# A hybrid decoder layer: three more places for raw weights in the seven-product passes, the sums of weights in the convolution's buffers, and a plain pair first

## The chip, the cores and the metric

The kernel runs on one core of one Trainium2 chip. The core's engines each work through a queue of their own in order: TensorE (PE in the profile, its weight loads PEld), VectorE (DVE), ScalarE (ACT), GpSimd (POOL) and SyncE (SP), which here issues nearly all transfers from memory. They are kept in step by semaphores. The metric is the device time of one execution in microseconds, and fewer is better. Three runs of the kernel before gave 1087.1, 1087.87 and 1090.15 us; the median is 1087.87 us.

## The reference

One decoder layer on 256 tokens of width 2048, all in float32. A token mixer (two groups of attention heads and an output projection) comes first; its code is not touched. Then comes the channel mixer, where the change lies:

```python
h = rmsnorm(x, pre_ffn_g[l])
u = causal_dwconv(h @ w_up[l], conv_w[l], conv_b[l])      # w_up 2048 x 11264, conv of width 3
gate, val = jnp.split(u, 2, axis=-1)
y = (jax.nn.gelu(gate, approximate=True) * val) @ w_down[l]   # w_down 5632 x 2048
x = x + rmsnorm(y, post_ffn_g[l])
```

## The kernel before, in words

**Precision.** A float32 matrix is split into a high part (`whi`, a cast by ACT) and a low part (`wlo`, the difference, by DVE), both in the 32-bit format that PE multiplies at full pace. A product of float32 matrices is then three matmuls: high by high, high by low, low by high. A weight comes in by DMA as a `raw` tile of 128 x 1024 (512 KB). There are five such places, taken in turn; a load can be issued only when the last reader of the place's former weights is done. There are likewise five places each for `whi` and `wlo`, free again when PE has read them.

**The channel mixer** runs in two halves of 2816 columns (22 tiles of 128, `FHALF`). In each half the up-projection (`proj_T4`, L272 to L290) makes, 11 times, a pair of tiles of the gate and a pair of the value. `conv` turns each into a convolved tile: ACT copies half of the PSUM bank (L881), DVE adds the other (L882), POOL multiplies with a row of scales (L883), ACT makes the last tap (L885), DVE adds the two others (L887, L889). ACT takes the GELU of the gates (L1033), DVE multiplies gate and value (L1040), and the product is split into `G` (L312 on ACT, L313 on DVE). These buffers (`u`, `cs`, `yg`, `yv`) are separate tiles, taken in turn.

**The seven-product passes** (`fast_pass`, L953 to L1012) multiply `G` by 1024 columns of `w_down`. There are three: two in half 0 (columns 0 to 1023, then 1024 to 2047) and one in half 1 (columns 0 to 1023). A pass has 11 pairs of rows of weights, each pair two loads, `ra` and `rb`. A pair is a 2 x 2 block of tiles by a 2 x 2 block of columns (`left`, `right`), so a plain pair takes eight products, 24 matmuls of 512 columns. The pairs 0, 2, 4 and 6 (`FAST`) are done with seven products, 21 matmuls, over sums of blocks. For these DVE makes `t13` and `t24` in the tile `tb` from `ra` and `rb` with four subtractions (L983, L984, L987, L989), and four parts are then split: half of `ra`, `t13`, `t24` and `rb`. A plain pair needs two splits. PE's matmuls all stand in L951. The eight PSUM banks of a pass are called `early` (four sums of products, done after the last fast pair, added to `y_sb` by `add_early`) and `late` (the four blocks that plain pairs also add to, taken out by `add_late`).

`tb` lies before the change in the room of `gbc` (free) in half 0, and in half 1 in the room of `hT`, which PE reads until the end of the up-projection. The vector `gbc_ffn` (1 MB, needed when the last columns are taken out) lies in `gbc`.

**After the passes** of half 1 come the columns 1024 to 1535 of that half and at last 1536 to 2047, both with three matmuls per product (L309), and the final norm.

**What sets the order.** PE's queue is in the order of the program text. On the other engines a scheduler places the instructions at build time by what they depend on and an estimate of when that is done. Each queue is strict at run time: an instruction that waits holds up all behind it, on SP too.

Of the kernel before, what the change touches and what calls it, by code (L numbers as in the profile page):

```python
# [8 lines left out]
F32 = mybir.dt.float32  # L9
# [8 lines left out]
P = 128  # L18
S = 256
D = 2048  # L20
# [11 lines left out]
def hybrid_layer(ctx: ExitStack, tc: tile.TileContext, x, pre_mix_g, w_in, b_forget, sinks,  # L32
# [814 lines left out]
    with tc.tile_pool(name="ffn", bufs=1) as fp:  # L847
# [23 lines left out]
        ubuf = [fp.tile([P, 258], F32, tag=f"u{i}", name=f"u{i}") for i in range(NU)]  # L871
        for u in ubuf:
            pool.memset(u[:, 0:2], 0.0)
        cnt = [0]
        y_sb = main.tile([P, 2, D], F32, tag="y", name="y_sb")

        def conv(b, ch, dst_tag):
            u = ubuf[cnt[0] % NU]
            cnt[0] += 1
            c = fp.tile([P, 256], F32, tag="cs", bufs=3, name="cs")  # L880
            act.copy(c, b[:, 256:512])  # L881
            dve.tensor_tensor(u[:, 2:258], b[:, 0:256], c, op=ALU.add)  # L882
            pool.tensor_tensor(u[:, 2:258], u[:, 2:258], rowf, op=ALU.mult)  # L883
            y = fp.tile([P, 256], F32, tag=dst_tag, bufs=4, name=dst_tag)
            act.activation(y, u[:, 2:258], AF.Identity, bias=cw[:, 3, ch:ch + 1],  # L885
                           scale=cw[:, 2, ch:ch + 1])
# [66 lines left out]
        def fast_pass(G, sums, k00, c0, tb, early, late, add_early, add_late):  # L953

            left, right = slice(0, 512), slice(512, UNIT)
            pairs = FHALF // 2
            plain = [u for u in range(pairs) if u not in FAST]
# [11 lines left out]
            for u in range(pairs):  # L969
                k = 2 * u  # L970
                ra, rb = (w_load(w_rows(w_down, k00 + k + a, 1, c0, UNIT), 1, UNIT)[0]
                          for a in range(2))
                if u in FAST:
                    i = FAST.index(u)
                    one, end = i == 0, i == len(FAST) - 1
# [7 lines left out]
                    dve.tensor_tensor(t13[:, left], ra[:, right], ra[:, left], op=ALU.subtract)  # L983
# [5 lines left out]
                    dve.tensor_tensor(t24[:, right], rb[:, left], t24[:, left],  # L989
                                      op=ALU.subtract)  # L990
                    f24 = parts(t24, UNIT)
                    b2 = parts(rb, UNIT)
                    product(m1, *of(k, 0), b11, left, one, end)
                    product(m5, *s_of(0), f13, left, one, end)
                    product(m7, *s_of(2), f13, right, one, end)
                    product(m6, *s_of(1), f24, left, one, end)
                    product(p4, *of(k + 1, 1), f24, right, one, False)
                    product(p2, *of(k + 1, 0), b2, left, one, False)
                    product(p3, *s_of(3), b2, right, one, False)
# [5 lines left out]
                end = u == pairs - 1  # L1005
                order2 = ([(a, x) for x in blocks for a in range(2)] if end else
                          [(a, x) for a in range(2) for x in blocks])
                for a, (bk, t, cols) in order2:
                    product(bk, *of(k + a, t), b[a], cols,
                            bk is p22 and u == plain[0] and a == 0, end and a == 1)  # L1010
# [5 lines left out]
        for half in range(2):  # L1016
            G = [fp.tile([P, 512], F32R, tag="G", bufs=FHALF, name=f"G{j}") for j in range(FHALF)]
            sums = None
            for g in range(FHALF // 2):
                c0 = (half * (FHALF // 2) + g) * 256  # L1020
                alt = (g + half) % 2
# [39 lines left out]
            tags = ("acc", "att") if half else ("att", "acc")  # L1061
            tb = (main.tile([P, 4, UNIT * 2], F32, tag="hT", name="tb")[:, 0:2, 0:UNIT] if half else
                  fp.tile([P, 2, UNIT], F32, tag="gbc", name="tb"))
            for n in range(0, 2 if half else 4, 2):
                early, late = ([bank(tag) for _ in range(4)] for tag in tags)
# [30 lines left out]
                fast_pass(G, sums, half * FHALF, n * 512, tb, early, late, add_early, add_late)  # L1096
# [34 lines left out]
        rest = main.tile([P, KT, 512], F32R, tag="hT", name="rest")  # L1131
# [4 lines left out]
        for u in range(FHALF // 2):  # L1136
            if u in (1, 2):
                sp.dma_start(x_back[:, u - 1, :], x_dram[(u - 1) * P:u * P, :])
            hi, lo = w_unit(w_rows(w_down, FHALF + u * 2, 2, 1536, 512), 2, 512,
                            keep=(None, [rest[:, c:c + 2, :].rearrange("p a c -> p (a c)")  # L1140
                                         for c in (4 * (u - LAST), 4 * (u - LAST) + 2)])
# [57 lines left out]
```

## Time and profile before

| what | value |
|---|---|
| median of three runs | 1087.87 us |
| the profiled execution, its own time | 1087.17 us |
| its span in the profile | 1085.4 us |
| PE busy | 1060.9 us, 98% of the span |
| DVE busy | 818.7 us, 75% |
| ACT busy | 630.8 us, 58% |
| POOL busy | 219.7 us, 20% |
| moved by DMA | 207.09 MB, mean 191 GB/s |
| mean granted clock of PE | 0.993 |

Between the span and the execution's own time lie 1.8 us. A busy PE is one that has a matmul under way, not one at its full pace: consecutive matmuls overlap in the records, so a lone matmul shows some 0.39 us where a stream of them takes 0.227 us for each.

### The profile page before, as it was taken

To read this page: it belongs to the slowest core of one execution; us is meant where nothing else is said; L and a number is where in the kernel's file an instruction comes from. 1 tells how busy PE (TensorE), PEld (TensorE's weight loads), DVE (VectorE), ACT (ScalarE), POOL (GpSimd) and SP (SyncE) were. 2 spreads that over 40 slices of the span, in tenths; PEclk is the share of its full clock that TensorE was granted. 3 is DMA by queue.
4 is the path that set the end of the run, shared out by engine and by line. 5 is a ranking of instruction groups with operands and counts; after the bars stand their busy time and mean duration, and the time that the engine had idled before them with its cause. 6 is when DMAs were issued, how large, how long until landed. Compare 5 with 4: busy or idle time off the path is not lost.

```text
span 1085.4 us, 16365 instructions
## 1 busy us (share of the span) xinstructions
PE 1060.9 (98%) x5950; PEld 919.6 (85%) x5950; DVE 818.7 (75%) x1336; ACT 630.8 (58%) x1087; POOL 219.7 (20%) x252
## 2 busy tenths in 40 slices
PE   8999999999999999999999999999999999989996
PEld 6899978887889888888888787888888888868886
DVE  5988878887568877778679887667877777588663
ACT  6766756667547756566565544455656565455550
POOL 3343243332022212121121000011212121100211
PEclk9999999999999999999999999999999999989998
DMA  8645556544862876566664655866666566457752
GB/s 287 207 123 172 175 155 211 166 149 155 306 220 80 290 216 190 181 197 191 193 194 152 195 175 186 298 187 186 191 198 191 179 198 191 135 160 225 278 171 78
DMA packets 157100, 207.09 MB, mean 191 GB/s; under 512 B 6844, under 2 KB 131036, under 8 KB 155996
## 3 DMA queue, kind: packets, MB, share of 16 engines
q1 hardware_dynamic: 156016, 203.37, 59.7%
q10 hardware_dynamic: 1004, 2.68, 0.6%
q8 instruction: 47, 0.77, 0.3%
q14 instruction: 33, 0.27, 0.1%
HBM read 201.68 MB, written 4.21 MB: 190 GB/s over the span
## 4 chain that ended last, share of the span: by engine, by line
PE 83%; DVE 7%; DMA 5%; issue 2%; ACT 2%; POOL 1%; SPq 0%; DVEq 0%; POOLq 0%; ACTq 0%
PE bank_acc L309 18%; PE bank_att L284 15%; PE bank_acc L284 14%; PE bank_att L290 8%; PE bank_acc L290 7%; PE bank_acc L253 5%; PE bank_att L951 5%; PE bank_acc L951 4%; DMA raw<-in_w_down_dram 3%; PE bank_acc L258 3%; DVE wlo L313 2%; DVE wlo L115 1%; PE bank_att L475 1%; PE bank_att L510 1%; PE bank_acc L916 1%
## 5 line engine op out<-in xcount | busy, mean ns | idle before, releaser
L115 DVE TENSOR_TENSOR wlo<-raw,whi 128x1024 fp32r<-128x1024 f32 (+3 forms) x291 | 358.4, 1241 | 136.9 <-ACT whi L112 132.7
L112 ACT CAST whi<-raw 128x1024 fp32r<-128x1024 f32 (+3 forms) x290 | 294.5, 1031 | 151.8 <-issue 91.9
L883 POOL TENSOR_TENSOR u<-u,rowf 128x256 f32<-128x256 f32 x88 | 95.5, 1105 | 497.3 <-DVE u L882 495.6
L284 PE MATMUL bank_att<-hT,whi 128*128 128x512 f32 x704 | 165.7, 390 | 0.0
L284 PE MATMUL bank_acc<-hT,whi 128*128 128x512 f32 x672 | 158.2, 390 | 0.0
L284 PEld LDWEIGHTS bank_att<-hT,whi 128*128 128x128 f32 x704 | 130.5, 188 | 26.3
L284 PEld LDWEIGHTS bank_acc<-hT,whi 128*128 128x128 f32 x672 | 124.5, 188 | 25.0
L253 PE MATMUL bank_acc<-hT,whi 128*128 128x512 f32 x352 | 89.2, 396 | 0.0
L290 PEld LDWEIGHTS bank_att<-hT,wlo 128*128 128x128 f32 x704 | 85.4, 188 | 1.9
L312 ACT CAST whi<-raw 128x1024 fp32r<-128x1024 f32 (+1 forms) x66 | 62.4, 973 | 41.9 <-PE bank_acc L951 14.8
L290 PE MATMUL bank_att<-hT,wlo 128*128 128x256 f32 x704 | 85.7, 279 | 0.0
L951 PE MATMUL bank_acc<-whi,G 128*128 128x512 f32 x264 | 84.7, 389 | 0.0
L290 PEld LDWEIGHTS bank_acc<-hT,wlo 128*128 128x128 f32 x672 | 81.6, 188 | 1.8
L309 PE MATMUL bank_acc<-whi,oT 128*128 128x512 f32 (+1 forms) x272 | 82.5, 380 | 0.0
L290 PE MATMUL bank_acc<-hT,wlo 128*128 128x256 f32 x672 | 82.1, 279 | 0.0
L313 DVE TENSOR_TENSOR wlo<-raw,whi 128x1024 fp32r<-128x1024 f32 (+1 forms) x66 | 73.2, 1132 | 9.3 <-ACT whi L312 9.3
L253 PEld LDWEIGHTS bank_acc<-hT,whi 128*128 128x128 f32 x352 | 62.9, 188 | 11.3
L951 PEld LDWEIGHTS bank_acc<-whi,G 128*128 128x128 f32 x264 | 49.6, 188 | 10.3
L309 PEld LDWEIGHTS bank_acc<-whi,oT 128*128 128x128 f32 x272 | 50.2, 188 | 9.3
L951 PE MATMUL bank_acc<-wlo,G 128*128 128x512 f32 x132 | 52.2, 395 | 2.9 <-DVE wlo L313 2.7
L309 PE MATMUL bank_acc<-whi,G 128*128 128x512 f32 (+1 forms) x196 | 51.8, 350 | 0.0
L309 PE MATMUL bank_acc<-wlo,oT 128*128 128x512 f32 (+1 forms) x136 | 51.2, 377 | 0.0
(249 smaller groups left out, 1664.7 us busy)
## 6 DMA issues: line engine op xcount, KB each, us to landing
raw<-in_w_up_dram SPq DMA_DIRECT2D x176, 512.0 KB, 3.9
raw<-in_w_down_dram SPq DMA_DIRECT2D x88, 512.0 KB, 5.0
raw<-in_w_in_dram SPq DMA_DIRECT2D x51, 512.0 KB, 4.0
raw<-in_w_out_dram SPq DMA_DIRECT2D x32, 512.0 KB, 5.0
raw<-in_w_in_dram SPq DMA_DIRECT2D x16, 384.0 KB, 3.4
cb<-c_dram SPq DMA_DIRECT2D x8, 256.0 KB, 3.7
x_sb<-in_x_dram SPq DMA_DIRECT2D x2, 1024.0 KB
x_dram<-x_sb ACTq DMA_DIRECT2D x2, 1024.0 KB
```

The source lines that it names most:

```text
L112: i1 = act.copy(hi[:, cs], raw[:, cs])
L115: i2 = dve.tensor_tensor(lo[:, cs], raw[:, cs], hi[:, cs].bitcast(F32), op=ALU.subtract)
L253: pe.matmul(b, parts[u][0][:, a, m * P:(m + 1) * P], hT[:, kt, :], start=(kt == 0), stop=(kt == KT - 1))
L258: pe.matmul(b[:, 256:512], parts[u][1][:, a, m * P:(m + 1) * P], hT[:, (v + u) * 4 + a, 0:256], start=False, stop=False)
L284: pe.matmul(b, parts[u][0][:, a, m * P:(m + 1) * P], hT[:, kt, :], start=(kt == 0), stop=(kt == KT - 1))
L290: pe.matmul(b[:, 256:512], parts[u][1][:, a, m * P:(m + 1) * P], hT[:, kt, 0:256], start=False, stop=False)
L309: pe.matmul(b, a, r[:, cols], start=(first and i == 0), stop=(last and i == 2))
L312: act.copy(hi, src)
L313: dve.tensor_tensor(lo, src, hi.bitcast(F32), op=ALU.subtract)
L475: pe.matmul(sb[e][:, cs], a[r, t * P:(t + 1) * P], b[r, 0:nk], start=(n == 0), stop=(n == 2))
L883: pool.tensor_tensor(u[:, 2:258], u[:, 2:258], rowf, op=ALU.mult)
L951: pe.matmul(b, a, r[:, cols], start=(first and i == 0), stop=(last and i == 2))
```

## The change

Six edits go together:

1. All of the convolution's buffers become slices of one tile `room` (4128 floats wide), taken up anew for each half by `conv_room`; `from_ring` deals them out in turn, as many of each as before.
2. When the convolutions of a half are done, the same room is taken up as `tb`, now three rows of 1024: two for `t13` and `t24`, the third a place for raw weights.
3. The room `gbc` becomes `extra`, two more places for raw weights. Of each eight loads of the passes the first five go to `raw`, then two to `extra` and one to `tb`.
4. The first pass of each half (`n == 0`) takes its pairs in the order 1, 0, 3, 2, 5, 4, 7, 6, 8, 9, 10. `first` finds for each bank which product starts it.
5. All passes use the `acc` banks for `early` and `att` for `late`; the alternation of banks in the up-projection of half 1 is shifted to suit.
6. `gbc_ffn` moves into the room of `hT`, and the held weights `rest` of the end move from there to `gbc` and `room`.

```diff
+        def conv_room():
+            room = fp.tile([P, ROOM], F32, tag="room", name="room")
+            ubuf[:] = [room[:, i * 258:(i + 1) * 258] for i in range(NU)]
+            for u in ubuf:
+                pool.memset(u[:, 0:2], 0.0)
+            at = NU * 258
+            for tag, n in (("cs", 3), ("yg", 4), ("yv", 4)):
+                rings[tag] = [room[:, at + i * 256:at + (i + 1) * 256] for i in range(n)]
+                at += n * 256
+
+        def from_ring(tag):
+            r = rings[tag]
+            r.append(r.pop(0))
+            return r[-1]
...
-            c = fp.tile([P, 256], F32, tag="cs", bufs=3, name="cs")
+            c = from_ring("cs")
...
-            y = fp.tile([P, 256], F32, tag=dst_tag, bufs=4, name=dst_tag)
+            y = from_ring(dst_tag)
...
-            for u in range(pairs):
+            for u in order:
                 k = 2 * u
-                ra, rb = (w_load(w_rows(w_down, k00 + k + a, 1, c0, UNIT), 1, UNIT)[0]
-                          for a in range(2))
+                ra, rb = (load(w_rows(w_down, k00 + k + a, 1, c0, UNIT)) for a in range(2))
...
+            if half:
+                conv_room()
             for g in range(FHALF // 2):
                 c0 = (half * (FHALF // 2) + g) * 256
-                alt = (g + half) % 2
+                alt = g % 2
...
-                gbf = fp.tile([P, D], F32, tag="gbc", name="gbc_ffn")
+                gbf = main.tile([P, 4 * D], F32, tag="hT", name="gbc_ffn")[:, 0:D]
                 sp.dma_start(gbf, post_ffn_g[0].partition_broadcast(P))
...
-            tags = ("acc", "att") if half else ("att", "acc")
-            tb = (main.tile([P, 4, UNIT * 2], F32, tag="hT", name="tb")[:, 0:2, 0:UNIT] if half else
-                  fp.tile([P, 2, UNIT], F32, tag="gbc", name="tb"))
+            extra = fp.tile([P, 2, UNIT], F32, tag="gbc", name="extra")
+            tb = fp.tile([P, 3, UNIT], F32, tag="room", name="tb")
+            spare = [extra[:, 0, :], extra[:, 1, :], tb[:, 2, :]]
+            loads = [0]
+
+            def load(src):
+                i = loads[0] % 8
+                loads[0] += 1
+                if i < 5:
+                    return w_load(src, 1, UNIT)[0]
+                sp.dma_start(spare[i - 5].rearrange("p (a c) -> p a c", a=1), src)
+                return spare[i - 5]
+
             for n in range(0, 2 if half else 4, 2):
-                early, late = ([bank(tag) for _ in range(4)] for tag in tags)
+                early, late = ([bank(tag) for _ in range(4)] for tag in ("acc", "att"))
+                order = list(range(FHALF // 2))
+                if n == 0:
+                    order[:8] = [1, 0, 3, 2, 5, 4, 7, 6]
...
-        rest = main.tile([P, KT, 512], F32R, tag="hT", name="rest")
+        rest = [fp.tile([P, 2, UNIT], F32R, tag="gbc", name="rest"),
+                fp.tile([P, ROOM], F32R, tag="room", name="rest")[:, 544:544 + 2 * UNIT]
+                .rearrange("p (a c) -> p a c", a=2)]
```

**How the queues change.** DVE at the start of the third pass (half 1), before: `u`, `yv` are the last convolution, `tb` and `wlo` the first fast pair (lines 983 to 989 the subtractions, 313 the splits). One split of that pair stands ahead of the end of the up-projection.

```order
L313 TENSOR_TENSOR wlo<-raw,whi 128x512
...
L983 TENSOR_TENSOR tb<-raw 128x512
L882 TENSOR_TENSOR u_3941<-bank_att,cs 128x256
L882 TENSOR_TENSOR u_3942<-bank_att,cs 128x256
L984 TENSOR_TENSOR tb<-raw 128x512
L987 TENSOR_TENSOR tb<-raw,tb 128x512
...
L1040 TENSOR_TENSOR yv<-yv,yg 128x256 x2
L313 TENSOR_TENSOR wlo<-tb,whi 128x1024
```

The same place now (898 to 905 are the convolution, 1004 to 1010 the subtractions):

```order
L313 TENSOR_TENSOR wlo<-raw,whi 128x1024
L313 TENSOR_TENSOR wlo<-raw,whi 128x512
L898 TENSOR_TENSOR room<-bank_acc,room 128x256 x2
...
L313 TENSOR_TENSOR G_7350<-room,G_7350 128x256
L1004 TENSOR_TENSOR tb<-raw 128x512
L1005 TENSOR_TENSOR tb<-raw 128x512
L1008 TENSOR_TENSOR tb<-raw,tb 128x512
L1010 TENSOR_TENSOR tb<-raw,tb 128x512
L313 TENSOR_TENSOR wlo<-tb,whi 128x1024 x2
L313 TENSOR_TENSOR wlo<-raw,whi 128x1024 x2
L313 TENSOR_TENSOR wlo<-extra,whi 128x1024
```

The splits of pair 1 and of half a `ra` now stand ahead of the last convolution, and all four subtractions behind the whole of it.

SP at the same place, with the end of the up-projection's loads (`raw<-in_w_up_dram`), one piece of the difference:

```order
-L69 DMA raw<-in_w_down_dram 128x1024 x21
-L1138 DMA x_back<-x_dram 128x2048
-L69 DMA raw<-in_w_down_dram 128x1024
-L69 DMA raw<-in_w_down_dram 128x2x512 x6
-L1138 DMA x_back<-x_dram 128x2048
...
+L1093 DMA extra<-in_w_down_dram 128x1024 x2
+L69 DMA raw<-in_w_up_dram 128x4x256 x87
+L69 DMA raw<-in_w_down_dram 128x1024 x7
+L1072 DMA gbc_ffn<-in_post_ffn_g_dram 128x2048
+L1093 DMA tb<-in_w_down_dram 128x1024
+L69 DMA raw<-in_w_down_dram 128x1024 x3
```

Two of the first eight weights are loaded an up-projection early, and `gbc_ffn` now stands in front of the load into `tb`.

DVE late in the first pass of half 0, now (the second row is the first subtraction of the second pass; the first row splits pair 6; 1109 and 1110 are `add_early`):

```order
L313 TENSOR_TENSOR wlo<-tb,whi 128x1024 x2
L1004 TENSOR_TENSOR tb<-extra 128x512
L313 TENSOR_TENSOR wlo<-raw,whi 128x1024 x2
L1109 TENSOR_TENSOR y_sb<-bank_acc,y_sb 128x512
L313 TENSOR_TENSOR wlo<-raw,whi 128x1024
L1110 TENSOR_TENSOR y_sb<-bank_acc,y_sb 128x512
```

The subtraction, which reads a weight of the next pass, stands ahead of the splits of this pass's pairs 8, 9 and 10.

More of the change, by code (lines that the diff above doesn't have):

```diff
@@ L951, in product, with fast_pass @@
                 pe.matmul(b, a, r[:, cols], start=(first and i == 0), stop=(last and i == 2))
-        def fast_pass(G, sums, k00, c0, tb, early, late, add_early, add_late):
+        def fast_pass(G, sums, order, k00, c0, load, tb, early, late, add_early, add_late):
             left, right = slice(0, 512), slice(512, UNIT)
-            pairs = FHALF // 2
-            plain = [u for u in range(pairs) if u not in FAST]
+            fast = [u for u in order if u in FAST]
             def of(k, t):
@@ L1008, in fast_pass @@
                 for a, (bk, t, cols) in order2:
-                    product(bk, *of(k + a, t), b[a], cols,
-                            bk is p22 and u == plain[0] and a == 0, end and a == 1)
+                    product(bk, *of(k + a, t), b[a], cols, first(bk), end and a == 1)
                     if end and a == 1:
@@ L1094, in add_late @@
                         dve.tensor_tensor(y_of(t, c), b, y_of(t, c), op=ALU.add)
-                fast_pass(G, sums, half * FHALF, n * 512, tb, early, late, add_early, add_late)
+                fast_pass(G, sums, order, half * FHALF, n * 512, load, tb, early, late, add_early,
+                          add_late)
             for n in range(2, 2 + half):
```

33 lines of the change are left out of this document (18 added, 15 removed).

## The prediction

> **What bounds the kernel now.** I read the head of the page first, then the chain of waits, then the stretches of the passes, and in them PE's waits and the queues it waits for.
>
> ```profile
> PE 1060.9 (98%) x5950; PEld 919.6 (85%) x5950; DVE 818.7 (75%) x1336; ACT 630.8 (58%) x1087; POOL 219.7 (20%) x252
> PE 83%; DVE 7%; DMA 5%; issue 2%; ACT 2%; POOL 1%; SPq 0%; DVEq 0%; POOLq 0%; ACTq 0%
> 681.89 23.80 PE bank_acc L951 x105
> 926.09 3.63 PE bank_att L284 x16
> 944.48 3.67 PE bank_att L284 x16
> ```
>
> The first two rows are from the page, the others from the chain. PE sets the end; nothing that the edit leaves PE to do shrinks, because the matmuls keep their number (1887 rows in PE's queue before and after). So the only gain is in what PE loses inside the passes. The third row gives the full pace: 23.80 / 105 = 0.2267 us for each matmul. A pass has 4 x 21 + 7 x 24 = 252, so it needs 57.12 us. The stretches of the three passes, with the matmuls of L951 alone:
>
> ```profile
> 585.07:644.57 59.50, 57.93 (x253) 47.06 (x253) 1.00 0.60 195
> 644.57:705.69 61.12, 58.69 (x253) 46.72 (x251) 1.00 0.67 223
> 947.97:1016.07 68.10, 61.99 (x252) 49.41 (x251) 0.92 0.66 218
> ```
>
> The length stands behind the colon pair; a matmul that crosses an edge counts on both sides. The losses are 59.50 - 57.12 = 2.38 us, 61.12 - 57.12 = 4.00 us and 68.10 - 57.12 = 10.98 us, together **17.36 us**. That is the ceiling of the gain. Three things make them up.
>
> The third pass loses its time at its start (PE, DVE, ACT and POOL by time):
>
> ```profile
> 948.42 0.39 PE L951 MATMUL bank_acc<-whi,G 128*128 128x512 f32 x1
> 952.57 0.49 PE L951 MATMUL bank_acc<-whi,sums 128*128 128x512 f32 x1 [3.77 <-ACT whi L312]
> 954.94 0.80 PE L951 MATMUL bank_acc<-wlo,sums 128*128 128x512 f32 x1 [1.88 <-DVE wlo L313]
> 959.57 0.63 PE L951 MATMUL bank_att<-whi,G 128*128 128x512 f32 x1
> 963.41 0.48 PE L951 MATMUL bank_att<-whi,G 128*128 128x512 f32 x1
> 948.17 0.69 DVE L983 TENSOR_TENSOR tb<-raw 128x512 f32<-128x512 f32 x1 [6.66 <-PE bank_att L284]
> 948.78 0.74 DVE L882 TENSOR_TENSOR u<-bank_att,cs 128x256 f32<-128x256 f32 x2
> 953.01 0.75 DVE L1040 TENSOR_TENSOR yv<-yv,yg 128x256 f32<-128x256 f32 x2
> 955.48 0.68 DVE L989 TENSOR_TENSOR tb<-raw,tb 128x512 f32<-128x512 f32 x1
> 956.09 0.68 DVE L983 TENSOR_TENSOR tb<-raw 128x512 f32<-128x512 f32 x1
> 947.99 0.65 ACT L881 COPY cs<-bank_att 128x256 f32<-128x256 f32 x2 [6.03 <-PE bank_att L284]
> 950.98 0.60 ACT L885 ACTIVATE yv<-u,cw 128x256 f32<-128x256 f32 x1 [0.44 <-POOL u L883]
> 949.27 1.68 POOL L883 TENSOR_TENSOR u<-u,rowf 128x256 f32<-128x256 f32 x2 [9.48 <-DVE u L882]
> ```
>
> `tb` lies in `hT` there, so DVE could not subtract until the up-projection ended (idle 6.66 us, released by PE), and then the first fast pair and the last convolution shared DVE. PE had three matmuls of that pair ready; the 22nd matmul of the pass starts at 963.41, where the pace would have had it at 947.97 + 21 x 0.2267 = 952.73. That is 10.68 of the 10.98 us.
>
> Part of it is the clock, in the stretches of this place (the column after the engines is the granted clock):
>
> ```profile
> 952.00:954.00 2.00, 0.49 (x1) 0.19 (x1) 2.00 (x6) 1.07 (x3) 0.00 (x0) 0.84 0.57 219
> 960.00:962.00 2.00, 2.00 (x6) 1.61 (x5) 2.00 (x3) 1.51 (x3) 0.00 (x0) 0.50 0.59 150
> 962.00:964.00 2.00, 2.00 (x7) 1.53 (x7) 2.00 (x3) 0.14 (x1) 0.00 (x0) 0.60 0.80 231
> 672.00:674.00 2.00, 0.59 (x4) 0.30 (x3) 2.00 (x3) 1.34 (x2) 0.00 (x0) 1.00 0.67 225
> ```
>
> After the gap of 3.77 us PE ran at half clock from about 953.4 (0.84 over 2 us is 0.64 us at half) to 963.6. A gap of 1.41 us at 672 left it whole.
>
> The second pass loses to the ring of five weights. From the chain, DVE's queue, and the times from issue to landing (620 to 706 us):
>
> ```profile
> 636.11 5.54 DMA raw<-in_w_down_dram
> 650.52 6.41 DMA raw<-in_w_down_dram
> 662.36 6.25 DMA raw<-in_w_down_dram
> 657.03 0.69 DVE L983 TENSOR_TENSOR tb<-raw 128x512 f32<-128x512 f32 x1 [3.66 <-DMA raw<-in_w_down_dram]
> 673.65 0.50 PE L951 MATMUL bank_acc<-wlo,G 128*128 128x512 f32 x1 [1.41 <-DVE wlo L313]
> DMA to landing us min/median/max: 3.7/5.2/9.5
> ```
>
> DVE frees a place, the load takes some 6 us, DVE waits for it, and twice PE waits for DVE. The stretch's DMA share is 0.67 and its engines average 223 GB/s, so it is the places, not the transfers, that are short.
>
> **The change part by part.** *Conversions, subtractions, matmuls, conv operations:* none added or removed; the same rows stand in other places. *Eight places:* five loads are 2.5 pairs of lead. At 45 matmuls for a fast and a plain pair (10.2 us) that is 12.8 us round the ring, of which a landing takes about 6. Eight are 20.4 us, with some 14 us left for DVE. DVE's work for the two pairs follows from starts in its rows: 0.61 us for a subtraction (955.48 to 956.09), 1.14 for a split of 1024 (3.41 us for three, below) and half of that for a split of 512:
>
> ```profile
> 647.09 3.41 DVE wlo L313 x3
> 345.00:350.00 5.00, 5.00 (x45) 5.00 (x44) 5.00 (x17) 5.00 (x16) 0.00 (x0) 1.00 0.00 0
> 948.00:960.00 12.00, 5.89 (x14) 3.48 (x13) 11.83 (x20) 7.32 (x12) 1.68 (x2) 0.72 0.12 44
> ```
>
> The first row is from the chain, the others are stretches. That is 4 x 0.61 + 0.57 + 5 x 1.14 = 8.7 us in 10.2. DVE keeps up when it does not wait, and I take the loss of the second pass from 4.00 to 0.5 us. Its bounds are 0 and 4.00 (if DVE's order and not the ring makes it). *Extra transfers:* none; the 2 x 512 KB that now go to `extra` before half 0 stand in SP's queue behind eight loads of `w_up`, where the transfers idle (0 GB/s in 345 to 350). The waits of that load, on POOL's and PE's last use of the mix's tiles, are over by then. In half 1 they take the place of `gbc_ffn`'s 1 MB ahead of the last loads of the second pass. `gbc_ffn` now goes out when PE is done with `hT`, at the start of the third pass, where the transfers moved 44 GB/s; it holds the load of `tb` and three behind it, but that load waits for the end of the convolution anyway. I cost these at nothing; uncovered, 1 MB at 218 GB/s is 4.8 us of transfers.
>
> *The start of a first pass* is where the change takes and gives. Now PE has a whole plain pair (24) and half of `ra` (3), split ahead of time, and one matmul on the high part of `t13`: 28 matmuls, 6.35 us of cover. Behind that PE needs the low part of `t13`. In the room `tb` shares with the convolution, DVE must first finish all of it. From the third pass's rows, counted from the end of the up-projection (T0 = 947.97): ACT's last `yv` ended at 951.58, T0 + 3.6; without the 0.6 us of subtraction ahead of `u` (L983 at 948.17), 0.4 earlier, T0 + 3.2, since the first copy ends at T0 + 0.4 anyway. Behind it stand one L887, one L889, two L1040 and the two splits of `G`, six of 0.33 to 0.47 us with ACT's cast between, 2.3 us: T0 + 5.5. Four subtractions, 2.4: T0 + 7.9. The split of `t13`, 1.14: T0 + 9.1. The next parts follow every 1.14 us and PE uses each for 6 matmuls (1.36 us), so PE is not held again: it wants pair 3's first low part at T0 + 13.4, and DVE has it after `t24`, `rb` and that split, at T0 + 12.6. The loss is 9.1 - 6.35 = 2.8 us, and 3.2 with some 0.1 us for each of the four hand-overs between engines. In the first pass POOL's two products took longer:
>
> ```profile
> 586.23 2.22 POOL L883 TENSOR_TENSOR u<-u,rowf 128x256 f32<-128x256 f32 x2 [8.49 <-DVE u L882]
> ```
>
> 2.22 us against 1.68, so I take 3.7 us there. This one is a *cost*: in half 0 `tb` was in a free room before, the first fast pair was split ahead and the pass lost only 2.38 us. The bounds of a start: 2.0 us (no hand-overs, POOL's products twice as fast) and 5.4 us (convolution as slow as it was among the subtractions, `G` done at T0 + 8.2).
>
> *Sum.* Losses now: 3.7 + 0.5 + 3.2 = 7.4 us against 17.36, a gain of 10.0 us. The profiled execution took 1087.17 us (span 1085.4 and 1.8 around it): 1087.17 - 10.0 = 1077.2. The median shown is 0.7 above that run, so **1077.9 us**.
>
> **A rule beside it.** The Trainium skill, TensorE: Matmul & The Clock Gate, Part 1, says that the array falls to half clock after an idle window of some 3.4 us that runs freely, and is whole again after a busy one. By that rule the gap of 3.77 us had to trip it and the one of 1.41 us not; the trace agrees with both. By it the new gap, which one matmul splits, leaves the sum as it is, unless a window may hold a matmul, as the one before 953.4 did.
>
> **The rivals.**
>
> *The clock falls at the new starts.* The new gap of 3.2 to 3.7 us is broken by one matmul; the old one of 3.77 us was not. If it falls, PE takes 0.427 us a matmul (nine from 959.57 to 963.41). A short fall of eight matmuls costs 8 x 0.2 = 1.6 us; one as long as the old (10.2 us) costs 5.1. Both starts: 1077.9 + 3.2 = 1081.1 to 1088.1; one: 1079.5 to 1083. For it: the gap is nearly as long, and the window from 950 to 953.4 also had a matmul in it. Against: the pieces are about 1.8 and 1.3 us, near the harmless 1.41, and behind them PE has work at hand, which it lacked before.
>
> *The second pass keeps its loss.* Its first subtraction stands in DVE's queue ahead of the splits of pairs 8 to 10 and waits for a load that waits for pair 6's splits. With DVE at 8.7 us for two pairs behind the slow start, that load goes out about 10.5 us before PE wants pair 8. Landing 6.3, subtraction 0.6 and split 1.1 make 8.0, so 2.5 us are to spare; at the longest landing seen, 9.5 us, PE waits 0.7. If the whole 4.00 stays: 1077.9 + 3.5 = 1081.4.
>
> *The starts cost less.* If POOL and DVE overlap better and each start loses 2.0 us: 1077.9 - 2.9 = 1075.0.
>
> *The convolution in one room becomes slower* (the other side). All its buffers are now one tile. Were accesses kept apart only by the tile, each of ACT's copies would wait for DVE's last read of the projection before. A projection lasts 11.03 us (926.09 to 948.15 are two) and the convolution behind it 7.6 (926.09 to the end of the splits of `G`, row below, at 933.7), so it decides from 3.4 us on; each 0.5 us beyond that is paid on 43 projections, 21.5 us, 1099 us. Against it: the waits in the queues' order are the same in kind and number as before.
>
> ```profile
> 932.97 0.75 DVE L313 TENSOR_TENSOR G<-yv,G 128x256 fp32r<-128x256 f32 x2
> ```
>
> **How the numbers follow.** Forecast as summed 0.58; the clock falls at one or both starts 0.22; the second pass keeps most of its loss 0.10; cheaper starts 0.06; slower convolution 0.04. What a measurement of this kernel can tell from no change is about 0.3%, 3.3 us. The first, third and fourth lie over 6 us below the median, and so does all but the worst of the second. Faster 0.89, same 0.07 (the long fall at both starts), slower 0.04. The range reaches from cheap starts with nothing lost in the second pass (1074.5) to the second pass's loss with a clock that falls once (1083.5).
>
> **What would show it right or wrong.** In the changed profile the third pass should last about 60.3 us, the second 57.6 and the first 60.8. PE should run 24 matmuls without a gap, then wait twice, on ACT's cast and DVE's split of `tb`, 3 to 4 us together, in both first passes. The second pass's waits of DVE on transfers should be gone. The granted clock stays at 1.00 in the first pass. The stretches of the up-projection (353 to 585, 705 to 948) should keep their lengths within 1 us. The forecast is wrong if a first pass loses over 6 us, if DVE's wait for a transfer of the next pass shows ahead of pair 8, or if PE waits inside the up-projection.

## The result and the profile after

| | before | changed |
|---|---|---|
| median | 1087.87 us (1087.1 to 1090.15, 5 runs) | **1077.63 us** (1077.36 to 1079.23, 5 runs) |
| profiled execution, its span | 1087.17, 1085.4 us | 1077.63, 1075.6 us |
| the three passes | 59.50, 61.12, 68.10 us | 60.45, 57.28, 62.20 us |
| lost in them against 57.12 each | 2.38, 4.00, 10.98 us | 3.33, 0.16, 5.08 us |

The ratio is 0.9905, with an interval from 0.989 to 0.992. 1077.9 us had been forecast.

The head of the changed kernel's page, and its chain by engine:

```profile
PE 1056.9 (98%) x5950; PEld 919.1 (85%) x5950; DVE 822.4 (76%) x1336; ACT 630.7 (59%) x1087; POOL 224.9 (21%) x256
PE 89%; DVE 4%; ACT 2%; DMA 2%; POOL 2%; issue 1%; SPq 0%; POOLq 0%; DVEq 0%; ACTq 0%
```

The counts of PE, DVE and ACT are those of before; PE's share of the chain has gone from 83% to 89%. The stretches of the three passes, with the matmuls of `product` alone (start and end, length, PE and its weight loads with their counts, granted clock, DMA share, GB/s):

```profile
584.05:644.50 60.45, 57.69 (x252) 47.23 (x252) 1.00 0.57 192
644.50:701.78 57.28, 57.28 (x253) 47.12 (x251) 1.00 0.63 211
944.06:1006.26 62.20, 59.44 (x252) 48.17 (x251) 0.97 0.63 219
```

The second pass runs at the pace of the matmuls. The other two lose at their starts. PE at both (by time, the wait and what ended it in brackets):

```profile
592.21 0.50 PE L967 MATMUL bank_acc<-whi,sums 128*128 128x512 f32 x1 [1.87 <-ACT whi L312]
593.59 0.50 PE L967 MATMUL bank_acc<-wlo,sums 128*128 128x512 f32 x1 [0.88 <-DVE wlo L313]
952.21 0.50 PE L967 MATMUL bank_acc<-whi,sums 128*128 128x512 f32 x1 [1.87 <-ACT whi L312]
953.60 0.71 PE L967 MATMUL bank_acc<-wlo,sums 128*128 128x512 f32 x1 [0.88 <-DVE wlo L313]
```

The two waits are the same to a hundredth of a microsecond at both starts; only the length of the fourth row's matmul differs, 0.71 against 0.50 us. DVE and POOL at the first of them (the pass begins at 584.05):

```profile
584.94 1.34 POOL L899 TENSOR_TENSOR room<-room,rowf 128x256 f32<-128x256 f32 x2 [8.43 <-DVE room L898]
588.76 0.98 DVE L313 TENSOR_TENSOR G<-room,G 128x256 fp32r<-128x256 f32 x2
591.71 0.69 DVE L1010 TENSOR_TENSOR tb<-raw,tb 128x512 f32<-128x512 f32 x1
592.32 2.42 DVE L313 TENSOR_TENSOR wlo<-tb,whi 128x1024 fp32r<-128x1024 f32 x2
```

The convolution is done at T0 + 5.7 (588.76 + 0.98 - 584.05), the subtractions at T0 + 8.35, and PE gets the low part of `t13` at T0 + 9.54 (593.59).

In the up-projection of half 1 nothing has moved. Changed:

```profile
701.78:944.06 242.28, 242.28 (x1409) 214.16 (x1408) 183.13 (x275) 139.31 (x219) 48.66 (x42) 1.00 0.62 189
```

Before (PE, weight loads, DVE, ACT, POOL):

```profile
705.69:947.97 242.28, 242.28 (x1409) 214.15 (x1409) 178.93 (x273) 137.61 (x216) 46.07 (x42) 1.00 0.61 185
```

In sum the passes lose 8.57 us instead of 17.36, a gain of 8.79. The two profiled spans differ by 9.8. The other 1.02 us lie ahead of the first pass, which begins at 584.05 instead of 585.07. They lie ahead of the channel mixer too: from its first matmul the up-projection of half 0 takes 232.22 us in both kernels, and it begins at 351.83 instead of 352.85. The code of the token mixer, which stands there, is not touched. In the kernels below the first pass began anywhere from 583.84 to 585.88, always 232.22 us behind the start of that up-projection, so I do not count this microsecond as an effect of the change.

### The profile page after: what moved, and what is told of

It is laid out like the page before. It is cut to its first block, busy times and chain, and to the rows that moved or that the text cites. A ratio compares the mean times of both kernels' runs of the same rounds, so it can differ in the third digit from the quotient of the medians.

```text
span 1075.6 us, 16358 instructions
## 1 busy us (share of the span) xinstructions
PE 1056.9 (98%) x5950; PEld 919.1 (85%) x5950; DVE 822.4 (76%) x1336; ACT 630.7 (59%) x1087; POOL 224.9 (21%) x256
## 3 DMA queue, kind: packets, MB, share of 16 engines
q10 hardware_dynamic: 1004, 2.68, 0.6%
## 4 chain that ended last, share of the span: by engine, by line
PE 89%; DVE 4%; ACT 2%; DMA 2%; POOL 2%; issue 1%; SPq 0%; POOLq 0%; DVEq 0%; ACTq 0%
PE bank_acc L309 18%; PE bank_acc L284 16%; PE bank_att L284 14%; PE bank_att L967 12%; PE bank_acc L290 8%; PE bank_att L290 7%; PE bank_acc L253 4%; PE bank_acc L967 3%; PE bank_acc L258 2%; DVE wlo L115 2%; PE bank_att L475 1%; POOL scr L442 1%; PE bank_att L510 1%; PE bank_acc L932 1%; DMA x_in<-in_x_dram 1%
## 5 line engine op out<-in xcount | busy, mean ns | idle before, releaser
L899 POOL TENSOR_TENSOR room<-room,rowf 128x256 f32<-128x256 f32 x88 | 99.4, 1150 | 393.1 <-DVE room L898 391.5
L284 PE MATMUL bank_acc<-hT,whi 128*128 128x512 f32 x736 | 173.3, 390 | 0.0
L284 PE MATMUL bank_att<-hT,whi 128*128 128x512 f32 x640 | 150.6, 390 | 0.0
L967 PE MATMUL bank_att<-whi,G 128*128 128x512 f32 x384 | 122.5, 389 | 0.0
L253 PE MATMUL bank_acc<-hT,whi 128*128 128x512 f32 x352 | 89.2, 396 | 0.0
L901 ACT ACTIVATE room<-room,cw 128x256 f32<-128x256 f32 x88 | 53.0, 602 | 60.1 <-POOL room L899 59.9
L967 PEld LDWEIGHTS bank_att<-whi,G 128*128 128x128 f32 x384 | 72.2, 188 | 15.1
L903 DVE SCALAR_TENSOR_TENSOR room<-room,cw 128x256 f32<-128x256 f32 x88 | 61.9, 703 | 19.4 <-ACT room L901 19.4
L967 PE MATMUL bank_att<-wlo,G 128*128 128x512 f32 x192 | 74.7, 389 | 0.0
L313 DVE TENSOR_TENSOR wlo<-raw,whi 128x1024 fp32r<-128x1024 f32 (+1 forms) x44 | 49.5, 1149 | 9.4 <-ACT whi L312 9.3
L312 ACT CAST whi<-raw 128x1024 fp32r<-128x1024 f32 (+1 forms) x44 | 42.4, 991 | 21.3 <-PE bank_att L967 15.9
```

Source lines behind the costliest of these rows:

```text
L253: pe.matmul(b, parts[u][0][:, a, m * P:(m + 1) * P], hT[:, kt, :], start=(kt == 0), stop=(kt == KT - 1))
L284: pe.matmul(b, parts[u][0][:, a, m * P:(m + 1) * P], hT[:, kt, :], start=(kt == 0), stop=(kt == KT - 1))
L312: act.copy(hi, src)
L313: dve.tensor_tensor(lo, src, hi.bitcast(F32), op=ALU.subtract)
L967: pe.matmul(b, a, r[:, cols], start=(first and i == 0), stop=(last and i == 2))
```

## The experiments

Losses are lengths of passes less 57.12 us. The first four kernels ran on one chip, the next four on another, the last two on a third; each ratio is to the kernel before on the same chip (medians 1089.12, 1088.7 and 1088.38 us).

| kernel | median, us | ratio to before, interval | losses of the passes, us |
|---|---|---|---|
| the order alone, five places, own rooms | 1081.35 | 0.9931 (0.9906 to 0.9956) | 2.87, 4.85, 4.64 |
| all but the order | 1092.07 | 1.0026 (1.0016 to 1.0037) | 11.63, 0.00, 10.15 |
| two plain pairs ahead | 1069.56 | 0.9828 (0.9809 to 0.9846) | 0.00, 0.42, 0.00 |
| matmuls put into the gap | 1076.52 | 0.9887 (0.9866 to 0.9909) | 3.32, 0.00, 3.34 |
| change with five places | 1083.85 | 0.9965 (0.9953 to 0.9977) | 3.36, 5.02, 3.37 |
| two plain pairs, five places | 1079.24 | 0.9916 (0.9891 to 0.9942) | 4.22, 0.00, 4.40 |
| two plain pairs again | 1069.85 | 0.9835 (0.981 to 0.9859) | 0.00, 0.00, 0.00 |
| the change again | 1078.57 | 0.9917 (0.9886 to 0.9948) | 4.92, 0.00, 3.35 |
| two plain pairs, six places | 1075.83 | 0.9882 (0.986 to 0.9904) | 3.52, 0.65, 2.59 |
| two plain pairs, seven places | 1070.29 | 0.9833 (0.9809 to 0.9858) | 0.00, 0.10, 0.00 |

Each of these kernels computes the whole reference.

**The order alone.** The kernel before, with the order of pairs and of banks from the change; the five places, the separate buffers of the convolution and `tb` stay.

```diff
-            tags = ("acc", "att") if half else ("att", "acc")
+            tags = ("acc", "att")
...
+                order = list(range(FHALF // 2))
+                if n == 0:
+                    order[:8] = [1, 0, 3, 2, 5, 4, 7, 6]
...
-            for u in range(pairs):
+            for u in order:
```

> The kernel before with the order of pairs (plain pair first in the first pass of each half) and its banks alone: five raw places, the sums of weights where they were (free room in half 0, the room of hT in half 1). Theory 1 (two separate causes: the start of a first pass, and the ring of five weights in the second pass): the second pass keeps its loss of about 4.0 us, the first stays at 2 to 2.5 us as before (its first fast pair was split ahead already), the third falls from 11.0 to 1 to 3.5 us, since 28 matmuls cover DVE; time about 1078.5 to 1080.5 us. Rival (the order of pairs alone makes the gain and the eight places idle): the second pass falls to about 0.5 us too, time 1076 to 1077.5 us.

1081.35 us. Its passes:

```profile
584.17:644.16 59.99, 57.73 (x252) 47.14 (x252) 1.00 0.57 186
644.16:706.13 61.97, 58.56 (x253) 46.72 (x251) 1.00 0.68 219
948.57:1010.33 61.76, 59.59 (x252) 48.09 (x251) 0.97 0.63 207
```

and DVE in its second pass:

```profile
657.38 0.69 DVE L989 TENSOR_TENSOR tb<-raw 128x512 f32<-128x512 f32 x1 [4.38 <-DMA raw<-in_w_down_dram]
669.31 0.69 DVE L989 TENSOR_TENSOR tb<-raw 128x512 f32<-128x512 f32 x1 [3.00 <-DMA raw<-in_w_down_dram]
```

The order alone takes 6.3 us from the third pass and nothing from the second, where DVE goes on waiting for loads. So the gain of the second pass comes from the places or the room. The third pass lost more than the 1 to 3.5 us that I had expected, and the time lies above my range: the clock fell in that pass, as shown below.

**All but the order.** The change with the pairs in their old order and the banks as before.

```diff
-                if n == 0:
-                    order[:8] = [1, 0, 3, 2, 5, 4, 7, 6]
...
-                early, late = ([bank(tag) for _ in range(4)] for tag in ("acc", "att"))
+                early, late = ([bank(tag) for _ in range(4)] for tag in (("acc", "att") if half else ("att", "acc")))
```

> The changed kernel with the pairs in the order 0 to 10 in every pass and the banks of before: eight places and the shared room without the plain pair first. Theory 1: the second pass loses under 0.5 us; both first passes start with 4 matmuls of cover against a low part that is ready 9.2 to 9.4 us after the up-projection, so each loses 8.5 us and some 1.7 us more for a clock that falls, 17 to 20 us in all; time 1087 to 1090 us, no gain over the kernel before. Rival (the order of pairs alone makes the gain and the eight places idle): the second pass loses 4 us as before, time 1091 to 1094 us.

1092.07 us, slower than before. PE at its first start:

```profile
593.75 0.80 PE L967 MATMUL bank_att<-whi,sums 128*128 128x512 f32 x1 [7.34 <-ACT whi L312]
595.14 0.79 PE L967 MATMUL bank_att<-wlo,sums 128*128 128x512 f32 x1 [0.59 <-DVE wlo L313]
```

With three matmuls at hand and one on the high part of `t13`, PE waits 7.34 and 0.59 us in the rows, 7.5 and 1.16 us by the spacing of its starts, and as long at the third pass. The low part comes at T0 + 9.57, where the change has it at T0 + 9.54; only the cover is shorter. With the room and without a plain pair to cover it, the two first passes lose 21.8 us, against 13.4 before; the second pass loses nothing here either. The time is that of the rival, 1091 to 1094, but its reason is not: the rival had the second pass lose 4 us. The starts cost more than the 17 to 20 us of the theory, because the clock fell for 10.24 and 6.83 us, where I had counted 1.7 us for each fall.

**Two plain pairs ahead.**

```diff
-                    order[:8] = [1, 0, 3, 2, 5, 4, 7, 6]
+                    order[:9] = [1, 3, 0, 5, 2, 7, 4, 8, 6]
```

> The changed kernel with two plain pairs first in the first pass of each half (pairs 1, 3, 0, 5, 2, 7, 4, 8, 6, 9, 10). Theory 1: 48 + 4 matmuls cover 11.8 us, more than the 9.4 us until the first low part, so the waits at the starts and the fall of the clock go; all three passes last 57.2 to 58 us, time 1068.5 to 1070.5 us. Rival (DVE's work for a fast and a plain pair is the bound as soon as the start is covered): PE waits come back later in the pass at the third or fourth fast pair, passes of 59 to 61 us, time 1073 to 1077 us.

1069.56 us, faster than either kernel. The cover is now 2 x 24 + 3 + 1 = 52 matmuls, 11.8 us. The low part is ready at T0 + 10.0 here, a little later than in the change; a split of half a `ra` stands among the convolution's operations on DVE. PE still has 1.8 us of work left then. The stretches:

```profile
585.56:642.68 57.12, 57.12 (x253) 47.28 (x252) 1.00 0.59 197
642.68:700.22 57.54, 57.41 (x253) 47.03 (x251) 1.00 0.64 209
942.66:999.78 57.12, 57.12 (x252) 47.11 (x251) 1.00 0.65 214
```

Three kernels, with 4, 28 and 52 matmuls ahead of the low part (0.9, 6.35 and 11.8 us), wait 8.7, 3.2 and 0 us there: each time the moment at which the low part is ready (T0 + 9.57, 9.54 and 10.0) less the cover, and nothing where the cover is longer. That is what the prediction's model of a start says.

**Matmuls put into the gap.** The change, with eight matmuls on a constant tile ahead of the first product over `t13`; they write the bank `m6`, which the first matmul of the pass's own products on that bank starts anew.

```diff
+                    if u == 0 and order[0] == 1:
+                        for _ in range(8):
+                            pe.matmul(m6, junk[:, 0:P], junk, start=True, stop=True)
                     product(m5, *s_of(0), f13, left, first(m5), end)
```

> The changed kernel with eight matmuls on a constant tile (into a bank that the next products start anew, so the result is not touched) in the gap between the half of ra and the first product over t13, in the first pass of each half. They fill 1.8 of the 2.0 us of the first piece of the gap. If the 1.9 us that the third pass lost beyond its wait are the clock: the granted clock stays at 1.00 there, the third pass lasts 60.4 to 60.7 us instead of 62.2, the first stays at 60.4; time about 1076 us. If they are DVE or the parts' places: third pass 62 us, time 1077.6 us. If the fillers delay the product behind them: both passes longer by up to 0.5 us.

1076.52 us. At its third pass (the record has seven of the eight matmuls):

```profile
951.12 1.90 PE L1017 MATMUL bank_acc<-junk 128*128 128x512 bf16 x7
954.53 0.50 PE L967 MATMUL bank_acc<-wlo,sums 128*128 128x512 f32 x1 [0.89 <-DVE wlo L313]
```

The product over `t13` starts no earlier, but both first passes now lose 3.3 us and the clock stays whole. So the change's extra 1.75 us in its third pass (5.08 - 3.33) goes with the clock; the waits are the same in both. The change again, below, has a third pass at whole clock, and it loses 3.35 us.

**The change with five places.** Everything as in the change, the room and the order too, but every load goes into the ring of five. The two loads into `extra`, which go out an up-projection early, fall away with the places.

```diff
-                i = loads[0] % 8
+                i = 0
```

> The changed kernel with five raw places instead of eight; shared room, early loads, order of the pairs and banks as in the change. Theory (the eight places are what took away the second pass's loss, the room in itself is free): the second pass loses 4 to 5 us again, as it did with five places and the changed order in the kernel before's rooms (61.97 us), the first and third stay at 60.4 and 60.4 to 62.2 us; 1077.6 + 4.5 = 1082, and so the same as that kernel (1081.35). Rival (the convolution in one room costs or saves time by itself outside the passes): the passes as above, but the time differs from 1081.4 by more than 2 us, and the difference lies in the stretches of the up-projection. Rival (the room and the early loads took away the second pass's loss, not the number of places): 1077.6, second pass under 58 us.

1083.85 us, 5.3 above the change on the same chip. Its second pass, and DVE in it:

```profile
646.36:708.50 62.14, 58.61 (x253) 46.74 (x251) 1.00 0.63 202
```

```profile
659.65 0.69 DVE L1004 TENSOR_TENSOR tb<-raw 128x512 f32<-128x512 f32 x1 [4.18 <-DMA raw<-in_w_down_dram]
671.68 0.69 DVE L1004 TENSOR_TENSOR tb<-raw 128x512 f32<-128x512 f32 x1 [3.10 <-DMA raw<-in_w_down_dram]
```

With eight places the only wait of DVE for a transfer in the two passes of half 0 is this one, in the change:

```profile
624.22 0.69 DVE L1004 TENSOR_TENSOR tb<-extra 128x512 f32<-128x512 f32 x1 [0.45 <-DMA extra<-in_w_down_dram]
```

So it is the added places that took the second pass's loss. The room by itself costs nothing outside the starts. This kernel's median lies 2.5 us above that of the order alone, on another chip and over the 2 us that I had set for a price of the room, but the rival's other condition is not met: the up-projections last as long in both (232.22 us in half 0; 242.43 and 242.44 in half 1). The 1.1 us between the two profiled spans (1080.9 and 1079.8) is less than the 1.7 us by which this kernel's first pass begins later (585.88 against 584.17), and that time lies ahead of the up-projection.

**Two plain pairs with five, six and seven places.** The fastest order, with `i = 0`, `i = loads[0] % 6` and `i = loads[0] % 7` in the same line.

> The first passes begin with two plain pairs as in the fastest kernel so far (1069.56 us, passes 57.1, 57.5, 57.1), but with five raw places. Theory (places and start are separate costs that add): the starts stay without a loss, since five places hold the two plain pairs and half of the first fast pair, and the second pass loses 4 to 5 us: 1069.6 + 4.5 = 1074. Rival (the ring falls behind only because a start throws DVE back, so without a loss at the start it stays ahead): 1069.5 to 1071, second pass under 58.5 us. Rival (five places also stall the first passes behind the two plain pairs, whose loads wait for the convolution's end): first and third pass 59 us or more, 1077 or more.

> Two plain pairs first, six raw places. With five the first and third pass lost 4.2 and 4.4 us (1079.24 us), with eight nothing (1069.85). At 10.2 us for four loads a place comes round after 12.8 us with five, 15.3 with six, 20.4 with eight; DVE's waits for a load were 3.90 and 2.59 us in the first pass with five. Theory (a sixth place brings each load forward by one load's time, 2.55 us): the waits fall to about 1.3 and 0, PE's loss to under 1 us in each first pass, 1070 to 1072. Rival (the loss falls evenly with each place, a third of 8.6 us for each): 1076 to 1077. Rival (only eight suffice): 1078 to 1079.

> Two plain pairs first, seven raw places. Theory (17.9 us round the ring, 11.6 of it for DVE and the queue, more than DVE's 8.7 us for two pairs, and 5.1 us more lead than with five): no loss, 1069.6, passes of 57.1 to 57.5 us. Rival (even fall, a third of 8.6 us left): 1072 to 1073. Rival (only eight suffice): 1078 to 1079.

1079.24, 1075.83 and 1070.29 us. The passes with five places, then from its chain the load that holds the first of them, and DVE behind that load:

```profile
583.84:645.18 61.34, 58.30 (x253) 47.00 (x252) 1.00 0.53 175
645.18:702.30 57.12, 57.12 (x253) 47.13 (x251) 1.00 0.69 221
944.74:1006.26 61.52, 58.30 (x252) 46.82 (x251) 1.00 0.63 209
```

```profile
599.78 6.72 DMA raw<-in_w_down_dram
606.59 0.69 DVE L1004 TENSOR_TENSOR tb<-raw 128x512 f32<-128x512 f32 x1 [3.90 <-DMA raw<-in_w_down_dram]
```

I had expected the price of five places in the second pass. It is paid in the first and third, 23 to 39 us behind their starts, and not at all in the second. The last rival has the time right, but not the place: the loads right behind the convolution's end hold nobody. DVE stands at the first subtraction of the third fast pair, with a split for the second one queued behind it, and PE waits for that split. The ring ran short in a first pass that had lost nothing at its start: here, in that of the order alone (2.87 us, from 613 on), and in that of the kernel before. Behind a start that waited 3.3 us the pass lost nothing more (five places in the change: 3.36 and 3.37). That the wait lets the loads come ahead is my reading of these losses; no run isolates it. Nor does it cover the second pass here, which loses nothing at its start and nothing later. Why that pass is spared in this kernel and not in the other two, the runs do not show.

With six places my theory (1070 to 1072) fell: 1075.83 us. With seven it held. The loss goes 8.6, 6.8, 0.1 us for five, six and seven: neither evenly nor by the 2.55 us of lead that I gave each place. The passes with six:

```profile
583.90:644.54 60.64, 58.59 (x252) 46.92 (x252) 1.00 0.53 176
644.54:702.31 57.77, 57.61 (x253) 46.96 (x251) 1.00 0.67 218
944.75:1004.46 59.71, 58.28 (x252) 46.81 (x251) 1.00 0.61 206
```

What makes the step between six and seven stays open.

**Both kernels again, side by side.**

> The fastest kernel so far once more, beside the five-place one and the changed kernel on one chip. Theory (the two plain pairs cover the end of the convolution whole): 1069.6, passes 57.1 to 57.5 us, about 8 us below the changed kernel of the same call (that kernel's losses of 8.6 less 0.5). Rival (part of the 8 us was the chip): less than 6 us apart.

> The changed kernel once more, unaltered. Theory (whether the clock falls at a start is chance in where the gap lies against the clock's windows): 1076 to 1079, gaps of about 1.9 and 0.9 us at both starts, the half clock at neither, one or both; each fall costs 1.4 to 1.75 us. Rival (the third pass's fall is fixed by the program): half clock for 3.41 us at the third pass's start again and whole clock in the first pass, passes of 60.4, 57.3 and 62.2 us.

1069.85 and 1078.57 us on one chip, 8.7 apart, about what the change still loses in its passes (8.57 and 8.27 us in its two profiles). The repeated change has the same gaps, but this time the clock fell in the *first* pass and not in the third (losses 4.92 and 3.35). Neither place is fixed by the program.

**When the clock falls.** The records of the granted clock answer this without another run. In each of the twelve profiles all changes of the clock lie on one grid: from the first, the rise near the start, to each later one there are whole multiples of 3.413 us, over spans of up to 1065 us (312 steps, two plain pairs with five places). The fall in all but the order at 164.24 and those at 590.91 and 959.55 are 125 and 108 steps apart. Where the grid lies against the program differs from run to run. So I cut the starts along each run's own grid; a stretch of the grid is called a window here. The change (PE's busy time in a window, with the matmuls of `product`, stands behind the window's length; the clock behind the weight loads):

```profile
588.49:591.90 3.41, 1.85 (x9) 1.19 (x7) 1.00 0.25 85
591.90:595.32 3.42, 2.23 (x9) 1.61 (x10) 1.00 0.61 208
950.30:953.72 3.42, 0.67 (x3) 0.31 (x3) 1.00 0.65 223
953.72:957.13 3.41, 3.41 (x9) 2.64 (x10) 0.50 0.32 109
```

The same waits of 1.87 and 0.88 us fell across two windows in the first pass, and into one in the third. The change again:

```profile
591.38:594.79 3.41, 1.68 (x6) 1.19 (x7) 1.00 0.72 245
594.79:598.20 3.41, 3.41 (x10) 2.66 (x9) 0.50 0.46 160
953.19:956.60 3.41, 1.87 (x7) 1.35 (x8) 1.00 0.68 245
```

The order alone, whose third pass has three small gaps and none over 1.1 us:

```profile
956.68:960.10 3.42, 1.73 (x7) 1.00 (x6) 1.00 0.02 5
960.10:963.51 3.41, 3.41 (x10) 2.63 (x9) 0.50 0.54 148
```

The change with five places, clock whole behind it:

```profile
955.48:958.90 3.42, 1.74 (x8) 1.12 (x6) 1.00 0.00 0
```

At the starts of the passes the clock fell behind windows in which PE was busy 0, 0.49, 0.67, 1.68 and 1.73 us, and stayed whole behind 1.74, 1.85, 1.87 and all busier ones. So the line is near half a window. Busy time is a rough measure of it, since a lone matmul counts 0.39 us and one in a stream 0.227, and the hundredth between 1.73 and 1.74 decides nothing. In all but the order:

```profile
590.91:594.32 3.41, 0.56 (x1) 0.29 (x1) 0.50 0.45 154
594.32:597.73 3.41, 2.81 (x7) 2.10 (x7) 0.50 0.45 156
597.73:601.15 3.42, 3.42 (x9) 2.64 (x9) 0.50 0.66 211
```

The half clock outlasts a window that is 2.81 us busy, and ends behind a full one (elsewhere 2.94 us, in the third pass of the kernel before, did not end it, and 2.91, in that of all but the order, did). Since it changes on the grid alone, it lasts 3.41, 6.83 or 10.24 us and nothing between, but for the last fall, in which the program ends. The line is not one for the whole kernel, and busy time is not all that decides: in the attention stage, with other shapes of matmuls, the clock fell behind windows of 1.89 us (two plain pairs, 160.25 to 163.66) and 2.15 us (all but the order, 160.83 to 164.24), and stayed whole behind one of 2.15 us (the change, 158.41 to 161.82). The Trainium skill, TensorE: Matmul & The Clock Gate, Part 1, has a free-running window of about 3.4 us, and the grid agrees with that. It has the clock fall after an idle window; here windows with seven matmuls' records in them sufficed, and the measurement decides.

## Why the prediction was right, and where only its total was

**The second pass: 0.5 forecast, 0.16 measured.** The cause held: with five places in the changed order it loses 5.0 us (62.14), with eight nothing. The step on the ring had the right mechanism (a load that DVE waits for), but its arithmetic, 12.8 us round the ring against a landing and DVE's work, does not give the measured fall over five, six and seven places.

**The start: 3.2 forecast by cover and ready time, 3.2 measured** by the spacing of the starts (2.03 + 1.16), at both. The steps to it were T0 + 5.5, 7.9, 9.1 and 0.4 for hand-overs; measured 5.7, 8.35 and 9.54. In the first figure two errors offset each other. At the third pass, T0 = 944.06:

```profile
945.62 1.30 ACT L901 ACTIVATE room<-room,cw 128x256 f32<-128x256 f32 x2 [0.93 <-POOL room L899]
948.77 0.98 DVE L313 TENSOR_TENSOR G<-room,G 128x256 fp32r<-128x256 f32 x2
```

ACT's last tap ended at T0 + 2.9 and not 3.2, because POOL's two products took 1.34 us and not 1.68; the six operations behind it took 2.8 us and not 2.3. With 0.26 us more for the subtractions, this uses up the 0.4 us that I had put in for hand-overs. The three covers bear the model out.

**The first pass: 3.7 forecast, 3.33 measured.** The premium of 0.5 us for POOL's slower products was wrong. I had taken their 2.22 us, among the rows of before, for a property of the first pass. They now took 1.34 us there and 1.34 in the third pass. That it had to be a cost against before (2.38) was right. But the kernel before loses its time elsewhere in that pass, some 23 us behind the start, where DVE waits for a load and PE for DVE:

```profile
607.30 0.69 DVE L983 TENSOR_TENSOR tb<-raw 128x512 f32<-128x512 f32 x1 [2.99 <-DMA raw<-in_w_down_dram]
609.19 0.50 PE L951 MATMUL bank_att<-wlo,sums 128*128 128x512 f32 x1 [1.10 <-DVE wlo L313]
```

So the change took away a loss to the ring in this pass too and put one at the start in its place, which the prediction does not say.

**The third pass: 3.2 forecast, 5.08 measured.** This is the step that failed: the clock. I gave it 0.22 and priced the short fall at 1.6 us; it came, in its short form, and cost 1.75. My argument against it was that the pieces of the gap were each near a harmless 1.41 us. The length of a piece did not decide. At these starts the falls went with PE's busy time in a window whose place the program does not set, and with 1.87 and 0.88 us of waiting within 3.25 us the two can share a window. The two profiles of the change show one fall each, in different passes. I had also misread the kernel before: its gap of 3.77 us did not hold a whole window of its grid. The one behind which the clock fell has a matmul in it:

```profile
949.94:953.36 3.42, 0.49 (x1) 0.19 (x1) 1.00 0.40 144
```

So the rule beside the forecast's sum, of an idle window, did not require this fall, as I had said; the trace alone shows it.

**The sum.** 7.4 us of losses forecast, 8.57 measured, so a gain of 8.8 in place of 10.0. For the profiled execution 1077.2 us followed from the sum, and 1077.63 was measured: 1.2 us less gain, but 1.02 us from the earlier start of the first pass, and 0.26 us more around the span (2.03 against 1.77). Within the 8.57 us the fall of 1.75 us was offset in part by 0.34 us less in the second pass and 0.37 us less in the first. By my own rival one fall should have given 1079.5 us or more. So part of the agreement is luck, of one to two microseconds. The 0.7 us that I added for the median had no counterpart either, since the profiled run of the change is itself the median. The upper end of the range adds up to 1083.0 us (1077.9 + 3.5 + 1.6), not 1083.5.

**The other rivals.** That the second pass keeps its loss is refuted (57.28 us), and so are the cheaper starts (3.2 us of gap, not 2.0) and the convolution slowed by its common room (232.22 and 242.28 us for the up-projections in both kernels). The room does have its price, though at the starts: without the plain pair the kernel is slower than before, 1.0026 (1.0016 to 1.0037). I had counted that coupling in the third pass, but had not listed it as the way in which the places alone would lose.

**Costed at nothing, and so measured:** the load of `gbc_ffn`, which now goes out at the third pass's start, and the load into `tb` behind it:

```profile
944.25 0.33 SPq L1072 DMA_DIRECT2D gbc_ffn<-in_post_ffn_g_dram  x1
949.83 0.33 SPq L1093 DMA_DIRECT2D tb<-in_w_down_dram  x1
```

The second waits for the end of the convolution, as forecast, and neither start's waits of PE end with a transfer.

## What to carry to other kernels

Price a shared buffer by the time at which its first user has finished, less the work that the waiting engine has at hand: here some 9.5 us (10.0 with two plain pairs) less 0.9, 6.35 or 11.8 gave 8.7, 3.2 and 0 us, and one more pair of cover was worth nearly as much as the whole change. With five places the toll of the ring moved from pass to pass when the order changed, so count the passes together before calling one of them cured. A gap on PE shorter than a window of 3.41 us can still cost a window at half clock; here matmuls put into the gap kept the clock, and so did closing it.

## What the runs showed of the hardware that was not expected

The clock's changes lie on a grid of 3.413 us that runs through the whole execution and lies differently in each run, and at these starts it fell behind windows in which PE was busy for up to about half the time (up to 1.73 us) and not behind busier ones; in the attention stage busy time does not separate the two. The same program, with the same waits to 0.01 us, therefore lost 1.75 us more at the third pass's start in one profile and 1.57 us more at the first's in the next. This fits the spread of the runs: 1077.36 to 1079.87 us in nine of the change, 1076.19 to 1077.04 in the four with matmuls in the gap; that each of the longer ones had a second fall was not profiled.
